# Six changes to the order of VectorE's work in a two-layer transformer trunk

## The chip, the cores and the metric

The kernel runs on one core of one Trainium2 chip. The metric is the device time of one launch in microseconds (us). The kernel before takes 1472.25 us, the median of 3 runs (1472.05 to 1473.08).

## The reference

The program computes a trunk of two layers over 512 latent tokens and 256 context tokens of width 1024, in float32. Cut to what matters for the change:

```
for l in range(2):                                   # layer
    h = modulate(rmsnorm(x, norm1_g[l]), shift, scale)          # shift, scale, gate from c @ w_mod
    z = h @ w_in[l]                                             # q | k | v | u | g
    q = rope(rmsnorm(q, q_norm_g[l])) * 64**-0.5                # 8 heads of 64
    k = rope(rmsnorm(k, k_norm_g[l]))                           # 2 heads of 64
    attn = softmax(q @ k.T) @ v                                 # context sees context only
    g = group_layernorm(gelu(g))                                # 4 groups of 128
    gm = gelu(u) * (w_spatial[l] @ g + b_spatial[l])            # mixes 128 positions
    x = x + gate1 * (concat(attn, gm) @ w_out[l])
    h2 = modulate(rmsnorm(x, norm2_g[l]), shift2, scale2)
    x = x + gate2 * (square(relu(h2 @ w_ff1[l])) @ w_ff2[l])    # 1024 -> 4096 -> 1024
```

In the second layer the context only supplies k and v. The output is the latent stream.

## The kernel before, in words

**Three products for one.** TensorE works on operands that are rounded to a shorter format (fp32r). So every operand is kept as a high part `hi` (a copy in that format) and a low part `lo` (operand less `hi`), and a product is three matmuls: hi by hi, hi by lo, lo by hi. `split` (L220 to L222) makes the two parts: ScalarE copies (L221, `CAST`), VectorE subtracts (L222, `TENSOR_TENSOR`). It serves the weights, in tiles of 128x1024 with a ring of five, and, written out at other lines, the activations: V (L782), the gated mixer `gm` (L795), the softmax weights (L1055), the squared relu (L1179).

**Stages.** Per layer: the input projections (kv, the mixer's u and its four gate tiles g with their layer norm, then q), then attention with the output projection, then the feed-forward layer `ff1`/`ff2` in eight chunks. The second layer begins with the kv projection of the new tokens, which runs into the end of the first layer's feed-forward.

**What sets the order.** The kernel is a program for a scheduler that places each instruction in its engine's row. The code keeps a virtual time and a list of due times (`fl.defer(delay, function)`, delays in the table `PAR`): work such as transposing, mixing and the second matmul group of an attention tile is emitted when its due time has come. In the first layer's feed-forward the rows of VectorE and ScalarE follow the code's order (`manual_schedule`); elsewhere the scheduler decides from its own times. `tc.issue_after(x)`, wrapped as `behind(x)`, keeps an instruction behind another in the row. An engine works through its row in order, so an instruction that waits holds up all behind it.

**Lines that the change touches.**
- `qk` (L699 to L728) takes a PSUM bank with two tiles of q or k. ScalarE squares it (L706), VectorE sums the squares per head (L708, the *reduce*), multiplies the bank by the rotary cosines (L712) and, with halves exchanged, by the sines (L716, two instructions), and adds the two (L717; GpSimd in the second layer). L725 and `rsqrt` (L294 to L311) turn the sums into a factor, and L727 multiplies. After L716 nothing reads the bank any more.
- `make_gm` (L787 to L796) makes the two parts of `gm`. In the first layer the low parts (L795, 128x768) are kept behind the fourth attention tile's maximum (`maxes[3]`).
- `attn_tile`: scores into a `pa` bank, row maximum (L1036), exponential with row sums (L1041), transposes (L1052) and their split (L1054, L1055). After the last of four tiles the sums' reciprocal is taken at once (L1059), and GpSimd spreads it over 128 columns (L1062). It is used later, when the attention product leaves PSUM (L1083, L1085).
- `sink_g` (L878): a gate tile's statistics (`stats`, L888 to L891, then a power on GpSimd at L298), then in `rest` its scaling (L907, four instructions) and its split, then in `mixing` the matmuls and their eviction (L932). L829 and L833 are steps of the gelu of another tile, and L833 is the last reader of that tile's bank.
- `pump` (L238) issues a weight tile's load and both parts of its split; `take` (L284) hands the tile to its user.
- `gate` (L981 to L986) adds a projected bank, times the modulation's gate, to the residual stream X, and thereby frees the bank.
- `ff1_first` and `relu2` (L1169 to L1179): relu and square on ScalarE (L1172, L1177), the square in full precision and its low part on VectorE (L1178, L1179).
- The norms (`Norm`): ScalarE squares X (L477), GpSimd or VectorE adds up (L479), TensorE sums over partitions (L488), `rsqrt`, VectorE copies (L510), TensorE spreads (L515), VectorE multiplies (L526) and takes the low part (L522). `N111` is the due time of the spreading in the second layer's second norm, latter group.

PSUM is held in three pools of banks, `pa` (two banks wide), `pb` and `pt`. A matmul into a bank waits until the last reader of its previous content is done.

## Time and profile before

| | |
|---|---|
| median of 3 runs | 1472.25 us |
| the profiled execution | 1474.03 us |
| span of that execution on the core | 1471.9 us |
| granted TensorE clock | 0.998 |

The profile is of one execution; about 2.1 us of its time lie outside the span. Its rows name an engine, a line, an operation and its operands without the buffer numbers: `X<-pb,modT,X` at L986 is a gate. A row of the timeline has the start from the span's start, the duration, the shape and the count; a row with x2 covers two instructions that follow each other. What stands in brackets is the idle time ahead of the instruction and what ended it. [...]

### The profile page before, as it was taken

How to read it: one execution, taken by the hardware profiler on the slowest of the kernel's cores; microseconds unless marked ns; L12 is line 12 of the kernel's file. 1: busy time of each engine (PE TensorE's matmuls, PEld its weight loads, DVE VectorE, ACT ScalarE, POOL GpSimd, SP SyncE). 2: the span in 40 equal slices, each digit the busy share in tenths (PEclk: the TensorE clock that was granted, in tenths of full speed). 3: DMA queues.
4: the chain of work that ended last, by engine and by line, in shares of the span. 5: the costliest groups of instructions: out<-in, count | busy, mean ns of one | idle time of the engine just before them, and what ended most of it. 6: DMA issues, size and time to landing. Idle time of an engine off the chain costs nothing.

```text
span 1471.9 us, 21047 instructions
## 1 busy us (share of the span) xinstructions
PE 1440.3 (98%) x8178; PEld 1225.0 (83%) x8178; DVE 909.6 (62%) x1594; ACT 642.3 (44%) x1141; POOL 364.6 (25%) x304
## 2 busy tenths in 40 slices
PE   6999999999999999999999999999999999999998
PEld 2899787988888888888888889998889888888887
DVE  5857767778766565655556547777968554444443
ACT  3552546664545452433325234546865323232221
POOL 0323512222256461323324223274121000000000
PEclk9999999999999999999999999999999999999999
DMA  9322443101233343423333212212002322222221
GB/s 367 114 72 92 178 152 143 70 1 57 84 128 122 109 143 99 139 99 136 99 138 118 88 39 74 99 58 72 16 1 73 118 97 100 100 92 95 100 100 57
DMA packets 50083, 148.71 MB, mean 101 GB/s; under 512 B 5440, under 2 KB 6976, under 8 KB 49984
## 3 DMA queue, kind: packets, MB, share of 16 engines
q1 hardware_dynamic: 49408, 146.72, 28.5%
q8 instruction: 64, 1.05, 0.3%
q10 hardware_dynamic: 576, 0.66, 0.1%
q14 instruction: 35, 0.29, 0.1%
HBM read 145.26 MB, written 2.10 MB: 100 GB/s over the span
## 4 chain that ended last, share of the span: by engine, by line
PE 86%; DVE 6%; ACT 3%; POOL 2%; issue 1%; DMA 1%; SPq 0%; POOLq 0%; ACTq 0%; DVEq 0%
PE pa L217 54%; PE pb L217 23%; PE pt L1052 3%; PE pb L354 2%; PE pt L217 2%; POOL m L298 1%; PE pt L745 1%; ACT w L1041 1%; DMA A<-in_w_mod 1%; POOL lo L222 1%; DVE lo L222 1%; ACT hi L221 0%; DVE s L907 0%; ACT A L1054 0%; DVE A L795 0%
## 5 line engine op out<-in xcount | busy, mean ns | idle before, releaser
L217 PE MATMUL pa<-A,hi 128*128 128x512 f32 (+2 forms) x1440 | 430.0, 376 | 0.7 <-DVE s L716 0.4
L221 ACT CAST hi<-raw 128x1024 fp32r<-128x1024 f32 x168 | 176.1, 1049 | 327.7 <-PE pa L217 246.1
L217 PEld LDWEIGHTS pa<-A,hi 128*128 128x128 f32 x1440 | 262.8, 188 | 46.8 <-DVE s L716 0.7
L217 PE MATMUL pa<-A,lo 128*128 128x512 f32 (+2 forms) x832 | 283.8, 347 | 0.0
L222 DVE TENSOR_TENSOR lo<-raw,hi 128x1024 fp32r<-128x1024 f32 x152 | 202.5, 1332 | 122.2 <-ACT hi L221 117.8
L403 POOL TENSOR_TENSOR C<-C,s 128x512 f32<-128x512 f32 x112 | 175.0, 1577 | 295.1 <-ACT s L402 288.3
L217 PE MATMUL pa<-B,hi 128*128 128x512 f32 x750 | 239.0, 391 | 0.0
L217 PEld LDWEIGHTS pa<-A,lo 128*128 128x128 f32 x832 | 156.7, 188 | 21.4
L986 DVE SCALAR_TENSOR_TENSOR X<-pa,modT,X 128x512 f32<-128x512 f32 x168 | 99.8, 615 | 105.6 <-PE pa L217 104.1
L217 PEld LDWEIGHTS pa<-B,hi 128*128 128x128 f32 x750 | 139.9, 188 | 27.1
L217 PE MATMUL pb<-B,hi 128*128 128x512 f32 (+1 forms) x600 | 157.0, 349 | 1.4 <-DVE X L986 1.0
L217 PE MATMUL pa<-B,lo 128*128 128x512 f32 (+1 forms) x450 | 155.2, 354 | 0.0
L986 DVE SCALAR_TENSOR_TENSOR X<-pb,modT,X 128x512 f32<-128x512 f32 (+3 forms) x116 | 70.9, 619 | 79.7 <-PE pb L217 79.7
L217 PE MATMUL pb<-hi,A 128*128 128x256 f32 (+1 forms) x608 | 118.1, 291 | 0.6 <-DVE m L725 0.6
L217 PEld LDWEIGHTS pb<-B,hi 128*128 128x128 f32 x600 | 104.4, 189 | 16.3 <-DVE X L986 2.2
L217 PE MATMUL pb<-B,lo 128*128 128x512 f32 (+1 forms) x300 | 104.2, 347 | 0.0
L217 PEld LDWEIGHTS pb<-hi,A 128*128 128x128 f32 x608 | 96.9, 191 | 2.2 <-PE pb L217 0.8
L217 PEld LDWEIGHTS pa<-B,lo 128*128 128x128 f32 x450 | 84.5, 188 | 14.9
L402 ACT ACTIVATE s<-k,silu 128x512 f32<-128x512 f32 x112 | 77.9, 717 | 34.4 <-DMA k<-in_w_mod 25.3
L217 PE MATMUL pb<-lo,A 128*128 128x256 f32 (+1 forms) x304 | 87.7, 288 | 0.0
L1055 DVE TENSOR_TENSOR A<-pt,A 128x384 fp32r<-128x384 f32 (+1 forms) x144 | 74.0, 537 | 14.6 <-ACT A L1054 12.6
L217 PE MATMUL pb<-A,hi 128*128 128x384 f32 (+2 forms) x288 | 80.4, 360 | 1.1 <-DVE s L833 0.6
(210 smaller groups left out, 2205.1 us busy)
## 6 DMA issues: line engine op xcount, KB each, us to landing
raw<-in_w_ff SPq DMA_DIRECT2D x128, 512.0 KB, 3.5
k<-in_w_mod SPq DMA_DIRECT2D x96, 256.0 KB, 2.8
raw<-in_w_tok SPq DMA_DIRECT2D x16, 512.0 KB, 3.5
raw<-in_w_out SPq DMA_DIRECT2D x16, 512.0 KB, 3.5
lo<-in_w_mod SPq DMA_DIRECT2D x16, 512.0 KB, 4.4
hi<-in_w_mod SPq DMA_DIRECT2D x16, 512.0 KB, 4.0
A<-in_w_mod SPq DMA_DIRECT2D x8, 512.0 KB, 9.9
B<-in_w_mod SPq DMA_DIRECT2D x8, 512.0 KB, 9.5
```

What stands on the lines that cost most here:

```text
L217: pe.matmul(out, a, b, start=start, stop=stop)
L221: act.copy(hi, src)
L222: (eng or vec).tensor_tensor(out=lo, in0=src, in1=hi.bitcast(F32), op=ALU.subtract)
L298: pool_e.tensor_tensor(out=y, in0=v, in1=mhalf[:, 0:n], op=ALU.pow)
L354: pe.matmul(ps[q:q + 32, :], S32[:, k, :], ws_[k2 // 2][:, k2 % 2 * 512:(k2 % 2 + 1) * 512], start=k < ns, stop=k >= KT - ns)
L402: act.activation(p, w, AF.Copy, scale=s)
L403: pool_e.tensor_tensor(out=a, in0=a, in1=p, op=ALU.add)
L745: pe.transpose(p[:, o:o + 128], stk[:, t, hh, c0:c0 + 128].bitcast(F32), ident)
L986: vec.scalar_tensor_tensor(out=xs, in0=src[:, s - off:e - off], scalar=modT[l][:, i * 8 + m, cond:cond + 1], in1=xs, op0=ALU.mult, op1=ALU ...
L1041: act.activation(p, ps[:, 0:nk], AF.Exp, bias=nmx, accum_out=sm)
L1052: pe.transpose(tp_[:, (kt - k0) * 128:(kt - k0) * 128 + 128], p[:, kt * 128:kt * 128 + 128], ident)
L1055: vec.tensor_tensor(out=ptl[:, k0:k0 + step, d], in0=src, in1=pth[:, k0:k0 + step, d].bitcast(F32), op=ALU.subtract)
```

## The change

It changes the order in which work is written or due, and no instruction's operation or shape. VectorE has 1475 rows before and after.

1. `qk`: the products with cosines and sines come first; the reduce over the squares and then the addition follow.
2. `make_gm`, first layer: the low parts are kept behind the eviction of the fifth mixing (`evicted[4]`) instead of the fourth maximum.
3. `attn_tile`: reciprocal and spreading become a function `factors`, due 1200 later.
4. `sink_g`, second layer: of gate tiles with an even number only the statistics are taken at once; scaling and split wait until the next tile, of odd number, is sunk.
5. Weight splits: while `state["gated"]` holds (from the end of a layer's attention to the end of its output projection, and in the first layer's last `ff2` chunk), the copy is issued at once and the low part is put on a list; each `gate` issues one from the list behind itself. `take` issues the low part of its own tile if it is still on the list. `out` weights are excepted.
6. `N111` goes from 3900 to 4600.

```
-       ... "N111": 3900.0 ...
+       ... "N111": 4600.0 ...
...
-            if held is None:
+            if held is None and state.get("gated") and "%s%d" % key[:2] not in PAR["WP"]:
+                act.copy(hi, raw)
+                pend.append((key, lambda hi=hi, lo=lo, raw=raw: vec.tensor_tensor(out=lo, in0=raw, in1=hi.bitcast(F32), op=ALU.subtract)))
+            elif held is None:
                 split(hi, lo, raw, pool_e if "%s%d" % key[:2] in PAR["WP"] else vec)
...
     def take(*key):
+        while any(k == key for k, _ in pend):
+            pend.pop(0)[1]()
...
             ss = small(2 * nh)
-            vec.tensor_reduce(out=ss.rearrange("p (a b) -> p a b", b=nh), in_=sq, axis=AX.X, op=ALU.add)
...
-                (pool_e if l in PAR['R1'] else vec).tensor_tensor(out=t1, in0=t1, in1=t2, op=ALU.add)
+                turning = t2
...
+            vec.tensor_reduce(out=ss.rearrange("p (a b) -> p a b", b=nh), in_=sq, axis=AX.X, op=ALU.add)
+            if tp < 2:
+                (pool_e if l in PAR['R1'] else vec).tensor_tensor(out=t1, in0=t1, in1=turning, op=ALU.add)
...
-                with behind(maxes[3] if l == 0 and len(maxes) > 3 else None):
+                with behind(evicted.get(4) if l == 0 else None):
...
+                elif l and n % 2 == 0:
+                    first()
+                    waiting.append(rest)
+                    fl.defer(PAR["G%d" % l], mixing)
                 else:
+                    while waiting:
+                        waiting.pop(0)()
                     rest()
...
-                    vec.scalar_tensor_tensor(out=xs, in0=src[:, s - off:e - off], ...)
+                    g = vec.scalar_tensor_tensor(out=xs, in0=src[:, s - off:e - off], ...)
+                    if pend:
+                        with behind(g):
+                            pend.pop(0)[1]()
...
                 if hh == qt == 1:
-                    rv = small(4, tag="rv", bufs=2)
-                    vec.reciprocal(rv, st["sm"])
-                    ...
+                    fl.defer(1200.0, factors)
...
+        state["gated"] = True
         with region('aend%d' % l):
             ...
+        state["gated"] = False
...
                 elif end:
+                    state["gated"] = True
                     more(96)
```

Line numbers in the rows of the kernel after are its own: L712, L716, L708, L717 and L725 are now L716, L720, L729, L731 and L732; L795 is L802, L829 and L833 are L836 and L840, L907 is L914, L932 is L939, L1055 is L1071, L1059 is L1080, L1172 and L1177 are L1192 and L1197. The low part of a gated weight is L273.

**VectorE in the first layer's attention over the context.** Before, with the low parts of `gm` (L795) ahead of an eviction of the mixing (L932):

```order
265 L1055 TENSOR_TENSOR A7_324_1904<-pt_325_1905,A6_323_1903 128x2x128
266 L1059 RECIPROCAL rv_333_1945<-sm_292_1804 128x4
267 L891 TENSOR_SCALAR m_341_1970<-mv_340_1961 128x4
268 L795 TENSOR_TENSOR A0_373_2077<-C0_100_482,A0_373_2077 128x768
269 L795 TENSOR_TENSOR A1_374_2080<-C0_100_482,A1_374_2080 128x768
270 L932 SCALAR_TENSOR_TENSOR s_331_1936<-pt_330_1923,gnh_41_173,k2_5_96 128x256 x2
```

and after:

```order
266 L898 TENSOR_SCALAR m_1964<-mv_1955 128x4
267 L1080 RECIPROCAL rv_1997<-sm_1804 128x4
268 L939 SCALAR_TENSOR_TENSOR s_1936<-pt_1923,gnh_173,k_5_96 128x256 x2
269 L1071 TENSOR_TENSOR A_324_1904<-pt_1940,A_323_1903 128x2x128
270 L1102 TENSOR_TENSOR mix_1945<-pb_1946,pv_1951 64x256
271 L442 TENSOR_TENSOR modT_90<-pt_1972,c_70 128x8
272 L1052 TENSOR_REDUCE m_1981<-pa_1978 128x1
273 L1052 TENSOR_REDUCE m_2013<-pa_2010 128x1
274 L914 TENSOR_SCALAR s_1793<-s_1793,mv_1955,m_1966 128x128 x4
275 L367 STREAM_TRANSPOSE s_2029<-pb_1986 128x512
276 L802 TENSOR_TENSOR A_373_2077<-C_100_482,A_373_2077 128x768
```

The eviction now follows the reciprocal directly; the first low part stands eight rows further on, behind a transpose (L362 before), and the second one further still.

**VectorE in the second layer's projections.** Before, with the scaling of a gate tile (L907) ahead of the last step of another tile's gelu (L833):

```order
1005 L891 TENSOR_SCALAR m_8853<-mv_8844 128x4
1006 L222 TENSOR_TENSOR lo_8997<-raw_8994,hi_8996 128x1024
1007 L907 TENSOR_SCALAR s_8838<-s_8838,mv_8844,m_8855 128x128 x4
1008 L833 SCALAR_TENSOR_TENSOR s_8937<-s_8937,pb_8864 128x512
1009 L222 TENSOR_TENSOR B_1498_8861<-s_8838,B_1498_8861 128x512
```

and after:

```order
1005 L898 TENSOR_SCALAR m_8853<-mv_8844 128x4
1006 L222 TENSOR_TENSOR lo_8997<-raw_8994,hi_8996 128x1024
1007 L840 SCALAR_TENSOR_TENSOR s_8930<-s_8930,pb_8857 128x512
1008 L914 TENSOR_SCALAR s_8838<-s_8838,mv_8844,m_8855 128x128 x4
1009 L895 BN_STATS bn_8942<-s_8930 128x6 x2
```

The gelu's step, which frees the bank, has moved ahead of the four scalings.

**ScalarE at the start of the first layer's feed-forward**, where `ff1_first` ends: relu and square of the rows m = 2 (`B2`) and m = 3 (`B3`), and copies of the high parts of weights. Before:

```order
365 L221 CAST hi_882_4379<-raw_881_4377 128x1024
366 L221 CAST hi_887_4425<-raw_886_4423 128x1024
367 L1172 ACTIVATE w_884_4410<-pa_874_4293 128x512
368 L1172 ACTIVATE w_885_4418<-pa_875_4294 128x512
369 L1177 ACTIVATE B2_864_4171<-w_884_4410 128x512
370 L1177 ACTIVATE B3_865_4172<-w_885_4418 128x512
371 L221 CAST hi_890_4431<-raw_889_4429 128x1024
```

and after:

```order
365 L221 CAST hi_882_4378<-raw_881_4376 128x1024
366 L1192 ACTIVATE w_884_4409<-pa_874_4292 128x512
367 L221 CAST hi_887_4424<-raw_886_4422 128x1024
368 L1197 ACTIVATE B2_864_4170<-w_884_4409 128x512
369 L1192 ACTIVATE w_885_4417<-pa_875_4293 128x512
370 L671 DMA w_893_4436<-in_rope 128x256
371 L1197 ACTIVATE B3_865_4171<-w_885_4417 128x512
```

A weight's copy has moved between the relu and the square of m = 2, and that square now stands ahead of the relu of m = 3. The load of the rotary table (L666) has moved up with it. On TensorE, 22 of the 24 matmuls by which `ff1` takes tile m = 4 to the latent columns stood right behind the first four matmuls of `ff2`; they now stand behind the first two row blocks of `ff2`.

## Prediction, made before the changed kernel ran

> **What bounds the kernel now.** I read the page's busy shares first, then what TensorE waited for, then the timeline at each wait that the change can reach. On the page (engine, busy us, share of the span, instructions):

> ```profile
> PE 1440.3 (98%) x8178; PEld 1225.0 (83%) x8178; DVE 909.6 (62%) x1594; ACT 642.3 (44%) x1141; POOL 364.6 (25%) x304
> ```

> TensorE is busy for 1440.3 of 1471.9 us, so no more than 31.6 us of idle time can be had from any reordering. The list of TensorE's waits (line, what it waited for, total us, times, longest) says which of it belongs to VectorE:

> ```profile
> PE pb L354 <- DMA A<-in_w_mod: 12.0, 1, 12.0
> PE pt L367 <- DVE s L932: 1.8, 1, 1.8
> PE pb L217 <- DVE X L986: 1.0, 2, 0.5
> PE pb L217 <- DVE m L725: 0.6, 1, 0.6
> PE pt L1052 <- DVE modT L437: 0.6, 1, 0.6
> PE pb L217 <- DVE s L833: 0.6, 1, 0.6
> PE pa L217 <- DVE A L522: 0.5, 1, 0.5
> PE pa L217 <- DVE s L716: 0.4, 1, 0.4
> PE pt L745 <- DVE m L309: 0.4, 1, 0.4
> PE pb L217 <- DVE s L716: 0.2, 1, 0.2
> ```

> Of the 31.6 us, 12.0 are the first load. The nine VectorE rows here add up to 6.1 us, and a few smaller ones are left out. That is roughly the prize. No operation is removed, so VectorE's work is the same in sum: a wait goes only where VectorE has idle time to put the displaced work in.

> The sum is made against the profiled execution, 1474.03 us; the median of the runs is 1472.25, 1.8 lower, and the difference is carried over to the median unchanged. A measurement of this kernel can tell about 0.2% from no change, 2.9 us.

> **Part 1, products ahead of the reduce.** VectorE, ScalarE's square and TensorE at the first q bank (start, us, instruction, idle before):

> ```profile
> 140.49 0.59 ACT L706 ACTIVATE s<-pb 128x512 f32<-128x512 f32 x1
> 141.11 0.69 DVE L708 TENSOR_REDUCE m<-s 128x8 f32<-128x512 f32 x1 [1.18 <-ACT s L706]
> 142.31 0.75 DVE L716 TENSOR_TENSOR s<-pb,G 128x256 f32<-128x256 f32 x2
> 143.21 0.35 PE L217 MATMUL pb<-hi,A 128*128 128x256 f32 x1 [0.60 <-DVE m L725]
> ```

> VectorE sat idle for 1.18 us until the square was there, then reduced, and only then read the bank, which came free at 143.06; TensorE waited 0.60. The products need the bank, not the square. They can start when the square does, at 140.49, instead of 0.62 later behind its end and another 0.61 later behind the reduce's turn: the bank comes free 1.2 us earlier, twice what the wait needs. What is late next is the factor. Reduce and addition (0.6 each) now follow the products, so its chain starts at 143.06 - 1.2 + 1.2, as before, but with the addition already done; the wait at L745 (0.4) loses perhaps half. I take 0.6 + 0.2 here, 0.4 for the kv bank (`pa`, L716) and 0.3 for the q banks of the second layer (L716, 0.2, and a shorter one). Sum **-1.5**, bounds -1.8 (all the rows named L725, L716 and L745, 1.6, and a little more) and -0.8 (this q bank alone).

> **Part 2, gm's low parts.** In the context's attention:

> ```profile
> 172.40 2.38 POOL L222 TENSOR_TENSOR lo<-raw,hi 128x1024 fp32r<-128x1024 f32 x1
> 173.70 1.11 DVE L891 TENSOR_SCALAR m<-mv 128x4 f32<-128x4 f32 x1
> 174.72 2.06 DVE L795 TENSOR_TENSOR A<-C,A 128x768 fp32r<-128x768 f32 x2
> 176.71 0.86 DVE L932 SCALAR_TENSOR_TENSOR s<-pt,gnh,k 128x256 f32<-128x256 f32 x2
> 177.72 0.25 PE L367 MATMUL pt<-s,c 128*32 128x8 f32 x8 [1.79 <-DVE s L932]
> 187.53 0.18 DVE L1059 RECIPROCAL rv<-sm 128x4 f32<-128x4 f32 x1 [0.69 <-ACT w L1041]
> 188.62 0.30 PE L1052 MATMUL pt<-c,w 128*128 128x128 f32 x1 [0.56 <-DVE modT L437]
> ```

> TensorE waits 1.79 for an eviction that stands behind 2.0 us of low parts. Those gone, the eviction starts at 174.7 instead of 176.7, and the 1.79 goes whole. But both low parts (1.03 each) come back, eight and fifteen rows on. The first falls in a stretch in which VectorE waits for TensorE anyway. The second stands just ahead of the next eviction, where VectorE's idle time is 0.69; 0.34 is left over, and with the row maximum that moves with it I expect the wait at 188.62 to grow by 0.5. **-1.3**, bounds -1.8 (nothing comes back) and -0.8 (1.03 comes back).

> The row L891 also shows what such sums can miss: 1.11 us for four elements per partition, where the same form takes 0.16 elsewhere (below); it ended at 174.81, and a split on GpSimd ended at 174.78. [...]

> **Part 3 and the due time N111.** Reciprocals (0.18 us each) move by one or two rows and their two copies on GpSimd with them; the product that needs them is emitted a further 3100 to 9800 later. Cost nothing, since nobody waits for them; bounds ±0.3, half of the wait at 188.62, the nearest one.

> **Part 4, a gate tile's scaling.** In the second layer's projections:

> ```profile
> 932.97 0.16 DVE L891 TENSOR_SCALAR m<-mv 128x4 f32<-128x4 f32 x1
> 933.04 1.22 DVE L222 TENSOR_TENSOR lo<-raw,hi 128x1024 fp32r<-128x1024 f32 x1
> 935.16 1.11 DVE L907 TENSOR_SCALAR s<-s,mv,m 128x128 f32<-128x128 f32 x4 [0.90 <-POOL m L298]
> 936.19 0.68 DVE L833 SCALAR_TENSOR_TENSOR s<-s,pb 128x512 f32<-128x512 f32 x1
> ```

> L833 frees a bank for which TensorE waits 0.6 (list above). It stood behind four scalings that themselves waited 0.90 for GpSimd's power. Now it goes into that idle time: 0.90 + 1.03 earlier. The scalings come 0.6 later, and the mixing that needs them is due 22100 of virtual time on. **-0.55**, bounds -0.6 and -0.4.

> **Part 5, weight splits behind gates.** Four places, each with its own answer.

> End of the second layer's attention, and its neighbour in kind, the end of the first layer's feed-forward:

> ```profile
> 884.96 1.21 DVE L222 TENSOR_TENSOR lo<-raw,hi 128x1024 fp32r<-128x1024 f32 x1
> 886.62 0.38 PE L217 MATMUL pb<-B,hi 128*128 128x256 f32 x1 [0.46 <-DVE X L986]
> 1108.16 1.22 DVE L222 TENSOR_TENSOR lo<-raw,hi 128x1024 fp32r<-128x1024 f32 x1
> 1109.29 0.87 DVE L986 SCALAR_TENSOR_TENSOR X<-pb,modT,X 128x256 f32<-128x256 f32 x2
> 1109.82 0.39 PE L217 MATMUL pb<-B,hi 128*128 128x256 f32 x1 [0.52 <-DVE X L986]
> ```

> At both, a low part of 1.2 us stands in front of two gates whose banks TensorE needs. At 1109 the gates now come first, which takes the 0.52, and what follows on VectorE runs on earlier into the first `ff1` matmuls, where I put 0.2 on it: **-0.7**, bounds -1.2 (the other gates of that stage too, 1.0 in the list) and 0. At 886 the wait of 0.46 goes too, and perhaps the 0.5 at L522. But the displaced low part is followed, on TensorE, by two gated banks ahead of products that were cover before; that can cost as much as a split and two gates, 1.21 + 0.87 = 2.1. I take **0**, bounds -1.0 and +1.6.

> End of the first layer's attention: three splits move behind gates, and one of them (1.2 us) then stands in front of the next gate, with TensorE's bank behind it; in return every gate of the stage, and with them the norm, is no longer behind those splits. **0**, bounds -0.8 and +1.2, one split or two thirds of one either way.

> The start of its feed-forward is where I expect a loss, because the split that is left over moves TensorE's cover:

> ```profile
> 387.40 1.05 ACT L221 CAST hi<-raw 128x1024 fp32r<-128x1024 f32 x1 [6.87 <-PE pa L217]
> 388.36 1.08 ACT L1172 ACTIVATE w<-pa 128x512 f32<-128x512 f32 x2
> 389.32 0.63 ACT L1177 ACTIVATE B<-w 128x512 fp32r<-128x512 f32 x1
> 388.79 0.39 PE L217 MATMUL pb<-B,hi 128*128 128x512 f32 x1
> 389.02 0.48 PE L217 MATMUL pa<-A,hi 128*128 128x512 f32 x1
> 391.20 1.29 DVE L1179 TENSOR_TENSOR B<-w,B 128x512 fp32r<-128x512 f32 x2
> ```

> Matmuls of this size start 0.23 us apart (388.79 to 389.02). Before, tile m = 4 filled TensorE from 389.02 on, for 24 x 0.23 = 5.5 us, while relu and square of m = 2 and 3 were finished. Now eight matmuls stand between the end of `ff1_first` (four ahead of 389.02, so 388.1) and the first use of m = 2: TensorE gets there at 389.9. The square of m = 2 is delayed by the copy put in front of it (1.05): from 388.36 on relu (0.54), copy (1.05) and square (0.63) now follow each other, to 390.5 with some overlap, where it was 389.95. A wait of 0.6. Six matmuls and the first use of m = 2 later, at 392.1, its low part is needed, and this stands on VectorE behind that copy's own low part: 389.95 + 1.23 + 0.65 + 0.65 = 392.5, a wait of 0.4. **+1.0**, bounds 0 (the scheduler's rows are kept but copy and split come early enough) and +1.7 (m = 3 is late as well).

> **Sum:** -1.5 - 1.3 - 0.55 - 0.7 + 0 + 0 + 1.0 = -3.05. 1474.03 becomes 1470.98, and the median **1469.2 us**. With every bound at its good end it is 7.5 less than before, with every one at its bad end 2.8 more.

> **The rivals.**
> - *The gated splits cost nothing.* The three uncertain places come out at -1.0, -0.5 and 0: -1.5 - 1.3 - 0.55 - 0.7 - 1.0 - 0.5 = -5.55, 1466.7. For it: VectorE is busy 62% and has room; against: at 389 the cover really moves. Chance 0.24.
> - *Nothing comes of it.* TensorE is at 98%, VectorE's work is unchanged, and each wait removed turns up at the next place where VectorE is late, as half of part 2 does: about 1472.3. Against: at 143 and 934 VectorE stood idle at the very time (1.18, 0.90). Chance 0.15. [...]
> - *Splits behind gates collide with the norm's sums*, slower. After each gate comes a square on ScalarE and an addition on GpSimd. Where a split ran beside one, the addition took 1.40 instead of 0.74:

> ```profile
> 1110.42 0.74 POOL L479 TENSOR_TENSOR acc<-acc,s 128x256 f32<-128x256 f32 x1 [2.33 <-ACT s L477]
> 1111.67 1.40 POOL L479 TENSOR_TENSOR acc<-acc,s 128x256 f32<-128x256 f32 x1 [0.51 <-ACT s L477]
> 1111.25 1.23 DVE L222 TENSOR_TENSOR lo<-raw,hi 128x1024 fp32r<-128x1024 f32 x1 [1.09 <-ACT hi L221]
> ```

> Seven splits now stand behind gates, in three norms. If each lengthens its norm's chain by 0.66 and TensorE feels it, that is +4.6; with parts 1, 2 and 4 (-3.35) and the start of the feed-forward (+1.0) the total is +2.3, 1474.5. It decides from four such collisions on (2.6 against 2.35). Against: splits stood beside additions before, too. Chance 0.11.

> **How the numbers follow.** The forecast has 0.50; its own range is 1468.0 to 1470.5, and about half of it lies beyond the 2.9 us. Faster by over 0.2% (below 1469.3): 0.24 + 0.26 = 0.50. Slower by over 0.2% (above 1475.2): 0.07, the upper end of the last rival. Within: 0.43. The range takes in the first two rivals and the forecast and leaves out the far ends: 1465.8 to 1473.6.

> **What would show it.** In the profile after, the waits at L833's and L725's banks and at L367 should be gone from TensorE's list; the reduce should follow the products without 1.18 us of idle time; the wait at L1052 behind L437's should be about 1.1; and near 390 TensorE should wait about 0.6 and 0.4 where it had none. I am wrong if no wait stands there, if the banks after 886 wait for over 2 us, or if GpSimd's additions of 1.4 us lead to new waits at L488 or L515.

## The result, and the profile after

| | before | after |
|---|---|---|
| median | 1472.15 us (4 runs, 1471.73 to 1473.08) | 1483.08 us (4 runs, 1482.36 to 1483.90) |
| profiled execution | 1474.03 us | 1483.59 us |
| span of that execution | 1471.9 us | 1481.8 us |

The ratio is 1.0071, with an interval of 1.0058 to 1.0083: the change makes the kernel 10.9 us slower, where 3.05 less was forecast and the range ended at 1473.6. The page's busy line after:

```profile
PE 1441.9 (97%) x8178; PEld 1228.5 (83%) x8178; DVE 916.5 (62%) x1594; ACT 644.1 (43%) x1141; POOL 364.1 (25%) x304
```

The same 8178 matmuls, busy within 1.6 us of before. So of the 9.9 us that the span gained, 8.3 are time in which TensorE stood still (1481.8 - 1441.9 = 39.9 against 31.6 before) and 1.6 time in which it was busy with the same work for longer. TensorE's list of waits after (line, what it waited for, total us, times, longest), in part:

```profile
PE pb L359 <- DMA A<-in_w_mod: 12.3, 1, 12.3
PE pb L217 <- DVE X L999: 4.0, 2, 2.1
PE pt L752 <- DVE k L740: 2.5, 2, 2.0
...
PE pt L217 <- ACT e L221: 1.7, 1, 1.7
PE pt L217 <- DVE acc L222: 1.7, 1, 1.7
PE pt L426 <- DVE m L421: 1.4, 1, 1.4
...
PE pt L752 <- DVE m L314: 1.1, 1, 1.1
```

What the change aimed at is gone: no row for the eviction (L932, 1.8 before), the gelu's bank (L833, 0.6) or the q bank (L725, 0.6). But the six rows below the first are new or have grown, to 12.4 us in sum. Adding up every wait of 0.15 us or more behind the first 60 us of the timeline gives 13.0 us before and 19.8 after: **+6.7**.

Beside the waits there is the granted clock. Stretches of 10 us (from:to, length, TensorE busy and its instructions, clock), of after and then of before, all in which the clock was under 0.99, but for the kernel's last ones:

```profile
180.00:190.00 10.00, 6.52 (x38) 0.66 0.40 130
340.00:350.00 10.00, 7.92 (x39) 0.98 0.00 0
350.00:360.00 10.00, 10.00 (x51) 0.85 0.33 110
...
990.00:1000.00 10.00, 7.97 (x58) 0.91 0.16 53
1000.00:1010.00 10.00, 10.00 (x44) 0.92 0.15 52
```

```profile
20.00:30.00 10.00, 9.35 (x48) 0.83 1.03 410
170.00:180.00 10.00, 8.21 (x59) 0.91 0.80 308
180.00:190.00 10.00, 8.76 (x63) 0.92 0.47 165
```

What is missing from 1.00, times 10 us, comes to 3.4 + 1.7 + 1.7 = 6.8 after and 1.7 + 1.7 = 3.4 before: **+3.4**, each drop worth 1.7 or twice that, and each right behind a wait of TensorE.

That 6.7 + 3.4 = 10.1 comes so near to the 9.9 of the span is partly luck. The sum of waits leaves out the first 60 us, where they grew by another 1.1, while before's drop at 20 us lies there, behind a wait of 1.8 that stands in after too and brought no drop. And the half clock near 180 ran from 182.4 to 189.3, in part while TensorE stood. So in these two executions the clock accounts for something between the 1.6 of longer work and 3.4: about a third of the loss at most. Over all runs the mean granted clock was 0.994 to 0.995 after, and 0.999 in the 25 runs of the kernel before that were made beside the first experiments. The difference of some 0.004 is at most 5.9 us, or half of the 10.9.

One more row, of the load queue (SP's):

```profile
SPq L264 <- DVE lo L273: 205.0, 11, 79.4
```

A low part that is kept behind a gate also keeps its raw tile, one of two buffers into which weights are loaded. A long wait of this queue is no loss in itself: before, it stood 706.0 us for the low parts (L222) in all, once for 75.0, and after 520.6 for those and 205.0 for these. It matters where the loads run short. At the end of the first attention the queue issued two loads at 337.72 and 343.75 before. After, it issued none until 351.16, just behind a low part that ran at 349.87.

### The profile page after: what moved, and what is told of

It is laid out like the page before. It is cut to its first block, busy times and chain, and to the rows that moved or that the text cites. A ratio compares the mean times of both kernels' runs of the same rounds, so it can differ in the third digit from the quotient of the medians.

```text
span 1481.8 us, 21046 instructions
## 1 busy us (share of the span) xinstructions
PE 1441.9 (97%) x8178; PEld 1228.5 (83%) x8178; DVE 916.5 (62%) x1594; ACT 644.1 (43%) x1141; POOL 364.1 (25%) x304
## 3 DMA queue, kind: packets, MB, share of 16 engines
q8 instruction: 64, 1.05, 0.3%
## 4 chain that ended last, share of the span: by engine, by line
PE 84%; DVE 7%; ACT 3%; DMA 2%; POOL 2%; issue 2%; SPq 0%; POOLq 0%; ACTq 0%; DVEq 0%
PE pa L217 52%; PE pb L217 24%; PE pt L1068 3%; PE pt L217 2%; PE pb L359 2%; PE pt L752 1%; DVE lo L222 1%; DVE A L527 1%; DMA A<-in_w_mod 1%; POOL m L303 1%; POOL lo L222 0%; DVE X L999 0%; DMA hi<-in_w_mod 0%; DVE s L531 0%; ACT w L1057 0%
## 5 line engine op out<-in xcount | busy, mean ns | idle before, releaser
L217 PE MATMUL pa<-A,hi 128*128 128x512 f32 (+2 forms) x1440 | 430.1, 376 | 0.5 <-ACT A L532 0.3
L221 ACT CAST hi<-raw 128x1024 fp32r<-128x1024 f32 x157 | 164.5, 1049 | 322.1 <-PE pa L217 242.1
L217 PEld LDWEIGHTS pa<-A,hi 128*128 128x128 f32 x1440 | 262.8, 188 | 46.8 <-DVE A L527 0.5
L217 PE MATMUL pa<-A,lo 128*128 128x512 f32 (+2 forms) x832 | 283.9, 347 | 1.1 <-DVE lo L273 1.1
L222 DVE TENSOR_TENSOR lo<-raw,hi 128x1024 fp32r<-128x1024 f32 x141 | 191.0, 1354 | 122.9 <-ACT hi L221 118.9
L217 PE MATMUL pa<-B,hi 128*128 128x512 f32 x750 | 239.6, 392 | 0.3 <-DVE X L999 0.3
L217 PEld LDWEIGHTS pa<-A,lo 128*128 128x128 f32 x832 | 156.6, 188 | 23.0 <-DVE lo L273 1.5
L217 PEld LDWEIGHTS pa<-B,hi 128*128 128x128 f32 x750 | 139.7, 188 | 28.4 <-PE pa L217 0.6
L217 PE MATMUL pb<-B,hi 128*128 128x512 f32 (+1 forms) x600 | 158.4, 351 | 4.4 <-DVE X L999 4.0
L217 PE MATMUL pa<-B,lo 128*128 128x512 f32 (+1 forms) x450 | 155.3, 354 | 0.0
L217 PEld LDWEIGHTS pb<-B,hi 128*128 128x128 f32 x600 | 105.2, 190 | 19.2 <-DVE X L999 5.0
L217 PE MATMUL pb<-hi,A 128*128 128x256 f32 (+1 forms) x608 | 118.0, 291 | 0.1
L217 PE MATMUL pb<-B,lo 128*128 128x512 f32 (+1 forms) x300 | 104.7, 349 | 0.0
L217 PEld LDWEIGHTS pb<-hi,A 128*128 128x128 f32 x608 | 96.9, 191 | 1.7 <-PE pb L217 0.3
L217 PEld LDWEIGHTS pa<-B,lo 128*128 128x128 f32 x450 | 84.5, 188 | 14.8
L217 PE MATMUL pb<-lo,A 128*128 128x256 f32 (+1 forms) x304 | 87.6, 288 | 0.0
L1071 DVE TENSOR_TENSOR A<-pt,A 128x384 fp32r<-128x384 f32 (+1 forms) x144 | 73.9, 536 | 16.5 <-ACT A L1070 14.6
L217 PE MATMUL pb<-A,hi 128*128 128x384 f32 (+2 forms) x288 | 81.8, 364 | 0.0
```

The source lines that it names most:

```text
L217: pe.matmul(out, a, b, start=start, stop=stop)
L221: act.copy(hi, src)
L222: (eng or vec).tensor_tensor(out=lo, in0=src, in1=hi.bitcast(F32), op=ALU.subtract)
L1071: vec.tensor_tensor(out=ptl[:, k0:k0 + step, d], in0=src, in1=pth[:, k0:k0 + step, d].bitcast(F32), op=ALU.subtract)
```

## The experiments

All are compared with before on the same chip; the part's lines are those of the diff in front. Differences in us are those of the medians, 1472.92, 1473.03 or 1472.52 for before; the ratio's interval says how sure they are. I first ran the parts apart.

**Part 1 alone** (`qk`'s reduce and addition behind the products):

> The kernel before with part 1 alone (products ahead of the reduce in qk). Own-waits theory (each part brings waits of its own, and a TensorE wait of about 2 us also costs a stretch of half clock): the waits at the first q bank (0.60, 0.39) and the kv bank (0.45) go, but the chain of the factor is late by 1.05 there, by 0.45 at the kv bank and by 2.0 in the second layer's q bank, the last with about 1.7 of clock: +3.5 us, 1475.7. Interaction theory (no part alone is bad, only all together): within 1 us of 1472.2. One-culprit theory (the gated splits do it all): -1.5 us, 1470.7, as predicted.

1474.86, ratio 1.0015 (1.0006 to 1.0024): 1.9 us slower. TensorE's longest waits are 1.80 at 178 (the eviction, as before), 1.85 near 991 at the second layer's q transposes, and 1.06 near 146. The forecast for this part was 1.5 less.

**Part 2 alone** (`gm`'s low parts behind the eviction):

> The kernel before with part 2 alone (gm's low parts behind the fifth eviction). Own-waits theory: the wait of 1.79 goes and two of 1.74 come, both followed by half clock where one was: +0.5 of waits and +1.7 of clock, 1474.4. Interaction theory: within 1 us of 1472.2. One-culprit theory: -1.3 us, 1470.9.

1473.33, ratio 1.0005 (0.9995 to 1.0014): +0.4, no difference that can be told. The wait of 1.79 at the eviction is gone, and one of 1.80 stands at 182.8, for `acc` (L222). I come back to it below.

**Part 5 alone** (`gated` set in all its places, due time N111 as before):

> The kernel before with part 5 alone (weights' low parts behind gates). Own-waits theory: waits of 2.1 (with 1.7 of clock) at the end of the first layer's attention, 1.7 in its feed-forward, 0.9 net at its end and 0.7 net at the end of the second attention: +7.1 us, 1479.3. Interaction theory: at most +2. One-culprit theory: the whole +10.9, 1483.

1486.24, ratio 1.0085 (1.0069 to 1.0102): 13.3 us slower, more than the whole change. The longest wait, TensorE's and the gate that it waited for:

```profile
1125.80 0.80 PE L217 MATMUL pb<-B,hi 128*128 128x256 f32 x2 [3.69 <-DVE X L991]
```

```profile
1125.26 0.48 DVE L991 SCALAR_TENSOR_TENSOR X<-pb,modT,X 128x256 f32<-128x256 f32 x1
```

The gate stands behind the norm's rows (L531 and L527), which fill VectorE from 1118.62 to 1125.3, but for 0.65, with no split among them. Part 5 was to take splits out of the way of gates; it did, and the gates are later.

**Parts 3 and 4 and N111:**

> The kernel before with parts 3, 4 and N111 alone (reciprocal later, even gate tiles' scaling later, due time 4600). All theories: the wait of 0.55 at L833's bank goes and nothing comes: -0.55 us, 1471.6. If it is slower by over 1 us, part of the loss sits here.

1473.83, ratio 1.0007 (0.9998 to 1.0016): +0.9, no difference that can be told. The 0.56 at the gelu's bank is gone, as forecast; 1.24 at the second layer's q transposes (L745, near 988) and 0.89 near 1116 have come. Nothing is won in sum.

**Part 5, place by place.** Only at the end of the first attention (`state["gated"] = l == 0` ahead of that region, and nowhere else):

> Part 5 only at the end of the first layer's attention. Order theory (the splits' new rows make the scheduler move TensorE's work as well, so that TensorE comes to two output-projection banks before VectorE, in the midst of the norm's multiplies, has gated the banks they need): a wait of 2.1 near 349 with up to 1.8 us of clock, and 0.8 to 1.0 twice near 415 and 435 from the split that is left over: +2 to +5 us, 1474.9 to 1478. Split theory (a split in front of the gate makes it late): a split stands between the norm's multiplies and the late gate in the timeline. Clock rival (the loss is mostly the clock): the waits sum to less than a third of the loss.

1477.31, ratio 1.0030 (1.0020 to 1.0041): +4.3. Waits of 2.08 at 348, 0.99 at 413 and 0.81 at 432. Only at the end of the first feed-forward:

> Part 5 only at the end of the first layer's feed-forward. Order theory: 0.46 and 0.49 go, a wait of 1.9 comes for the first of two banks that TensorE reaches early: +0.9 us, and 0 to 1.7 of clock: 1473.8 to 1475.5. My prediction's term was 0.

1475.05, ratio 1.0016 (1.0006 to 1.0025): +2.0. The two waits of 0.46 and 0.48 near 890 are gone, and one of 1.89 for a gate has come. Only at the end of the second attention, with N111 at 4600:

> Part 5 only at the end of the second layer's attention, with N111 at 4600 as in the whole change. Order theory and prediction agree: the wait of 0.52 at the gates goes; -0.2 to -0.7, 1472.2 to 1472.7. With N111 at 3900 part 5 alone had a wait of 3.7 there (at 1125.80); if N111 is what saves it, no wait over 1 us is seen.

1474.74, ratio 1.0012 (1.0003 to 1.0021): +1.7. The 0.52 at the gates is gone, as forecast. The 3.69 is not there either, which I put down to the new due time, since part 5 is the same at this place. What came instead are 0.45 and 0.65 on low parts that TensorE now reaches too early (near 1123 and 1125), and 0.31. These waits, less those that went, are about half of the 1.7; the rest lies within the interval.

The single results of parts 1, 2 and 5 add up to 1.9 + 0.4 + 4.3 + 2.0 + 1.7 = 10.3, near the loss of the whole, 10.9; each is uncertain by 1 to 1.5 us, so that the agreement is better than it had to be. Some 8 us of it are part 5.

**Low parts kept back are let go at a region's end:**

```diff
             fl.run_fillers()
+            while pend:
+                pend.pop(0)[1]()
+        state["gated"] = False
```

> Part 5 alone, but the low parts that are still on the list are issued at the end of each layer's output projection instead of when their tile is taken. Load theory (the low part left over keeps one of the two load buffers and with it the queue of all loads, which makes the modulation late near 435): the waits near 415 and 435 (0.96 and 0.78) go, the others stay: 1.7 less than part 5 alone, 1484.5. Order theory alone: all waits stay, 1486.

This is part 5 as in the third experiment, and no low part outlives the end of an attention. 1480.87, ratio 1.0056 (1.0039 to 1.0073): +7.8 instead of +13.3. The waits near 413 (0.96 in the third experiment, for a gate) and 432 (0.78, for the modulation, L426) are gone; those of 2.08, 1.89 and 3.69 stay. So these two waits in the feed-forward come of a low part left over, and the big waits for gates do not. They are 1.7 of the 5.5 us won. A wait of 0.96 near 998 went too, and the half clock behind the 2.08, which stood in the profiled execution of the third experiment, does not stand in this one's; the two experiments also ran on different chips. The rest of the 5.5 is open.

**The gated weights' low parts at once, on GpSimd:**

```diff
+            if held is None and state.get("gated") and "%s%d" % key[:2] not in PAR["WP"]:
+                act.copy(hi, raw)
+                pool_e.tensor_tensor(out=lo, in0=raw, in1=hi.bitcast(F32), op=ALU.subtract)
```

> Part 5 at the end of the first attention, but with no low part kept back: GpSimd makes the low parts of the gated weights at once, VectorE makes none of them there. TensorE's order comes back to that of before but for one pair of matmuls, while VectorE has the run of modulated rows (L531, L527) in front of the gate of tile 4 without a split in between, as in the version with part 5. Theory 'TensorE's order': the wait of 2.08 was made by two output blocks that TensorE took earlier, with less cover behind them; here it is gone, no wait for a gate (X) is over 0.6 between 335 and 360 us, the waits of 0.99 and 0.81 near 412 and 432 go too, and the time is within 1.5 us of before. Rival 'VectorE's queue': the gate is late since it stands behind that run; then a wait of 1.5 to 2.1 stays and the time is 2 to 4 us above before. [...]

1478.21, ratio 1.0036 (1.0022 to 1.0050): 5.7 us slower, which neither of the theories had. TensorE's waits near the place, and VectorE's and GpSimd's rows at the second of them:

```profile
350.79 0.51 PE L217 MATMUL pa<-A,hi 128*128 128x256 f32 x2 [2.16 <-ACT hi L272]
363.06 1.02 PE L493 MATMUL pt<-ones,acc 128*128 128x1 f32 x8 [1.73 <-DVE acc L484]
```

```profile
360.00 2.37 POOL L273 TENSOR_TENSOR lo<-raw,hi 128x1024 fp32r<-128x1024 f32 x1 [0.71 <-ACT hi L272]
360.68 2.24 DVE L484 TENSOR_TENSOR acc<-acc,s 128x512 f32<-128x512 f32 x1 [0.83 <-ACT s L482]
```

No wait for a gate is left there. TensorE stands 2.16 us for a weight's copy, which stands behind norm rows on ScalarE (349.70, before 346.78). But its order has come back: 19 matmuls of `ff1` stand in front of the output block, as against 17 before and 7 with the low parts behind gates, although VectorE has the same run of norm rows. So TensorE's order follows the low parts, and not the norm rows. The run also shows the price of GpSimd: the addition L484 takes 2.24 us beside the split on GpSimd, against a median of 0.69 for it on VectorE in this run, and TensorE waits 1.73 for the sum. Behind each of the two waits the clock is 0.83 over 10 us, 3.4 us together, of the 7.7 by which this execution (1480.18) is above before's median.

**Part 1 in one layer alone** (the moved lines under `if l == 0`, then under `if l == 1`):

> Part 1 in the first layer alone. Theory 'scratch buffer in the second layer': the loss of part 1 is the wait near 990 us (1.85) where the reduce now stands behind a product that waits for a buffer GpSimd still reads; then this kernel is within 0.7 us of before, its waits near 140 to 190 adding up to about what they were. Rival 'late factor in the first layer': the wait of 1.06 at the transpose near 146 and of 1.00 near 185 carry it; then this kernel is 1.5 to 2.5 above before.

> Part 1 in the second layer alone; TensorE's order is word for word that of before, so all of the difference is VectorE's place. Theory 'scratch buffer in the second layer': a wait of 1.5 to 2 at the transpose (L747) near 990 us, released by the factor on VectorE, against 0.2 at the two places before; 1.5 to 2.2 us above before. Rival 'late factor in the first layer': that wait is made up for by the q banks that come free earlier; within 0.5 us of before.

First layer: 1473.12, ratio 1.0003 (0.9995 to 1.0012), +0.6. Second layer: 1474.49, ratio 1.0012 (1.0004 to 1.0021), +2.0, with TensorE's order that of before throughout. So the loss of part 1 is the second layer's. VectorE and TensorE there (start, us, instruction, idle before), and below them VectorE before:

```profile
987.04 0.76 DVE L718 TENSOR_TENSOR s<-pb,G 128x256 f32<-128x256 f32 x2 [2.66 <-POOL C L945]
987.71 0.68 DVE L730 TENSOR_REDUCE m<-s 128x8 f32<-128x512 f32 x1
988.42 1.10 DVE L733 TENSOR_SCALAR m<-m 128x8 f32<-128x8 f32 x1
989.44 0.68 DVE L741 TENSOR_TENSOR k<-w,k 128x512 fp32r<-128x512 f32 x1
...
990.17 1.09 PE L753 MATMUL pt<-c,k 128*128 128x128 f32 x8 [1.84 <-DVE k L741]
```

```profile
984.14 0.69 DVE L708 TENSOR_REDUCE m<-s 128x8 f32<-128x512 f32 x1 [0.29 <-ACT s L706]
...
987.49 0.76 DVE L716 TENSOR_TENSOR s<-pb,G 128x256 f32<-128x256 f32 x2 [2.06 <-POOL C L937]
988.17 0.58 DVE L725 TENSOR_SCALAR m<-m 128x8 f32<-128x8 f32 x1
988.66 0.68 DVE L733 TENSOR_TENSOR k<-w,k 128x512 fp32r<-128x512 f32 x1
```

In both kernels the product by the sines stands idle for over 2 us, until GpSimd's mixing (L937, L945 here) has read the scratch buffer that the product is to write. Before, the reduce ran ahead of that idle time and cost nothing. Now it follows it. (Some of these rows overlap the next by up to 0.09 us, as 987.04 + 0.76 and 987.71.) Between the start of the sine products and the end of `k`, for which TensorE waits, lay 988.66 + 0.68 - 987.49 = 1.85 us; now it is 989.44 + 0.68 - 987.04 = 3.08. The 1.2 more are the reduce (0.6) and a longer L733 (1.10 against 0.58). The sine products themselves also start later. Counted from 24 matmuls of TensorE (`pt<-ws,B`, at 978.88 here and 980.15 before), it is 8.16 us here and 7.34 before, 0.8 more, because GpSimd's split and with it the mixing ended that much later; why was not taken apart. (The idle times, 2.66 and 2.06, can't be compared, since before the reduce stood ahead of them.) Together that is 2.0, and the wait is 1.84. Another new wait of 0.81 stands near 1004, at the next transposes.

**TensorE halted on purpose.** The kernel before with 14 waits made in the second layer's feed-forward, where the clock is 1.00 and TensorE waits for nothing:

```diff
+                if m in HALT:
+                    d = tw([128, 512])
+                    for j, w in enumerate(HALT[m]):
+                        vec.tensor_copy(d[:, 0:w], ps[:, 0:w] if j == 0 else d[:, 0:w])
+                    halt.append(pe.transpose(pt()[:, 0:128], d[:, 0:128], ident))
...
+        with tc.issue_after(halt[-1].ins) if halt else nullcontext():
+            pe.matmul(out, a, b, start=start, stop=stop)
```

> The kernel before, with 14 halts of TensorE in the second layer's feed-forward, where it otherwise runs at granted clock 1.00 without a wait: after every second block of 24 matmuls VectorE copies a bank's 512 columns one to eight times, and a transpose that needs the copy stands in front of TensorE's next matmuls. By the copies' sizes the waits should run from about 0.5 to 4 us, most of them between 1.2 and 2.5. Theory 'half clock from 1.7 us on': behind most waits over 1.7 us the matmuls start 0.45 instead of 0.23 us apart for up to 3.4 us, behind those under 1.2 none do, so such a wait costs up to 1.7 us more than its length. Rival '3 us': only waits of over 3 us are followed by a half clock; then the drops seen at 180 and 350 in the changed kernel come from several waits close together, not from one. Rival 'chance': drops are as frequent behind short waits as behind long ones.

1531.69, in one execution; the waits are 40.7 of the 58.0 us by which the span is longer. Two of them, and what follows each:

```profile
1267.18 0.30 PE L1230 MATMUL pt<-c,w 128*128 128x128 f32 x1 [2.67 <-DVE w L1229]
...
1268.28 1.05 PE L220 MATMUL pa<-A,hi 128*128 128x512 f32 x2
1269.13 0.63 PE L220 MATMUL pa<-A,lo 128*128 128x512 f32 x1
...
1282.79 0.30 PE L1230 MATMUL pt<-c,w 128*128 128x128 f32 x1 [2.81 <-DVE w L1229]
...
1283.62 0.62 PE L220 MATMUL pa<-A,hi 128*128 128x512 f32 x2
1284.09 0.40 PE L220 MATMUL pa<-A,lo 128*128 128x512 f32 x1
```

Behind the 2.67 the matmuls start (1269.13 - 1268.28)/2 = 0.43 us apart, behind the 2.81 0.23. By wait: 0.39, 0.78, 1.14, 1.34 and 1.80 were followed by no drop; 2.67 by one; 2.81 once by none and once by one; 3.61, and 3.75 twice, by one of 3.41 us; 4.68, 5.14 and 6.07 each by one of twice that length, which began while the wait still ran. So, of these 14, the waits up to 1.8 were harmless and those from 3.6 on always cost; the rival of 3 us falls with the 2.67. But a wait that the kernel itself has near 184, of 1.53, was followed by half clock in the same run, so that 1.8 is no safe length.

In between, the two waits of 2.81 differ in how they lie. In the traces of before, of after and of this run the half clock, but for that at the kernel's end, comes in stretches of 3.41 us or twice that, and within one run their starts lie whole multiples of 3.41 us apart: 46 times in before (21.09 and 178.10), 49 and 190 times in after (182.43, 349.68 and 998.21), and here, with 1267.69, 1318.89, 1335.95 and 1373.50, 15, 5 and 11 times. Cut into such stretches, the time around the 2.81 near 1282 and around the other 2.81, near 1318, looks so (from:to, length, TensorE busy and its instructions, clock):

```profile
1277.93:1281.34 3.41, 2.05 (x10) 1.00 0.35 132
1281.34:1284.76 3.42, 1.97 (x9) 1.00 0.35 113
...
1315.47:1318.89 3.42, 0.61 (x4) 1.00 0.00 0
1318.89:1322.30 3.41, 3.41 (x9) 0.50 0.45 154
```

The first wait is shared by two stretches, and each keeps some 2 us of work. The second lies in one stretch, where 0.61 us of work are left, and the next one runs at half clock. Laid out in the same way, behind the first 60 us and without the kernel's end, these stretches at full clock have the least work: 1.62 in before (from 174.69), and 1.33 (346.27), 1.38 (994.80), 1.55 (899.23) and 1.61 (179.01) in after. All were followed by half clock but the one of 1.55, and no stretch with more work was. So in these two traces the work left in a stretch does not decide alone.

## Why the prediction was wrong

**Part 5, end of the first attention (forecast 0, bounds -0.8 and +1.2; measured +4.3).** The step that failed: I priced splits and gates on VectorE with TensorE's order as it was. I looked for moved cover (the work that fills TensorE until a gate has freed its bank) after 886 and at the start of the feed-forward, and not here. The cover moved here. TensorE and VectorE after, in front of the wait, and then before:

```profile
346.54 0.40 PE L217 MATMUL pa<-A,hi 128*128 128x256 f32 x2
346.77 0.28 PE L217 MATMUL pa<-A,lo 128*128 128x256 f32 x1
346.89 0.64 PE L217 MATMUL pa<-A,hi 128*128 128x256 f32 x4
349.61 1.18 PE L217 MATMUL pb<-B,hi 128*128 128x512 f32 x2 [2.08 <-DVE X L999]
```

```profile
341.70 0.86 DVE L531 SCALAR_TENSOR_TENSOR s<-X,A,pt 128x256 f32<-128x256 f32 x2
...
348.81 0.74 DVE L999 SCALAR_TENSOR_TENSOR X<-pb,modT,X 128x512 f32<-128x512 f32 x1
...
349.87 1.21 DVE L273 TENSOR_TENSOR lo<-raw,hi 128x1024 fp32r<-128x1024 f32 x1
```

```profile
346.56 0.40 PE L217 MATMUL pa<-A,hi 128*128 128x256 f32 x2
...
349.02 0.72 PE L217 MATMUL pb<-B,hi 128*128 128x512 f32 x2
```

```profile
348.22 0.74 DVE L986 SCALAR_TENSOR_TENSOR X<-pb,modT,X 128x512 f32<-128x512 f32 x1
```

Before, TensorE filled the time from 346.56 with 17 matmuls of `ff1` (`pa`) and took the next output block at 349.02, just when its bank came free. After, 7 matmuls stand there, and it is ready at 349.61 - 2.08 = 347.53, 1.49 earlier; and the gate is 0.59 later, for 15 of the norm's rows now stand in front of it where 11 and a split stood. 1.49 + 0.59 = 2.08.

Why the cover went can be read from the order of TensorE's row in the two built programs. Ten of the 17 matmuls now stand behind the output block. The first of them read two low parts and a high part of `ff1`'s weights. These two low parts are the ones that part 5 put behind the gates (L273, the first at 349.87, the second at 351.67), and the high part's load was issued only at 351.16. The others follow them in the row. So the work that had hidden the gate now needs what stands behind the gate. With the low parts made at once on GpSimd, 19 matmuls stood in front again. The waits of 2.08, 0.99 and 0.81 in the run of this place alone are 3.9 of its 4.3, and its profiled execution had no clock drop here.

**The like at 902 and 1126.** At 902 (895 in the run of that place alone; 1.89) all of the wait is lost cover. Counted from TensorE's same matmuls, the gate comes 7.13 us on in both kernels (890.72 to 897.85 before, 895.00 to 902.13 after), but of the matmuls that read the next weight tile 23 stood ahead of the block before, and 2 after. That tile's low part is now made at 903.58, behind the gate, and the others wait their turn behind its user. At 1126, without the new due time (3.69), the gate itself is late: counted from the first `ff1` matmul, it comes 4.15 us later in the third experiment (1121.11 to 1125.26), and 0.09 earlier before (1114.79 and 1114.70), while TensorE is ready for the block no earlier (1.00 us behind that matmul, 0.45 before). Why the norm's rows came ahead of the gate there was not taken apart.

**Part 5, end of the first feed-forward (forecast 0, measured +2.0) and end of the second attention (forecast -0.7, measured +1.7).** The waits named (0.46 and 0.48, 0.52) went. At 886 the upper bound, +1.6, was nearly right and the value taken was not. What failed there was the price of the moved cover, which I had seen: 2.1 at most, taken as 0. At the other end I had counted on a gain of 0.2 in the first `ff1` matmuls; there came waits of 0.45 + 0.65 + 0.31.

**Part 5, start of the feed-forward (forecast +1.0).** No wait stands near 390, so the step was too pessimistic about that place. The low part left over did its harm later: without it the waits of 0.96 and 0.78 near 413 and 432 were gone, 1.7 us.

**Part 1 (forecast -1.5, measured +1.9).** Two steps failed. The first: "The products need the bank, not the square." After, at the first q bank:

```profile
140.12 0.69 DVE L716 TENSOR_TENSOR w<-pb,G 128x512 f32<-128x512 f32 x1 [1.18 <-ACT s L711]
...
141.39 0.68 DVE L729 TENSOR_REDUCE m<-s 128x8 f32<-128x512 f32 x1
```

The very 1.18 us of idle time that the reduce had are now the product's, and the square ends them. All twelve cosine products wait on ScalarE in the built program, this one among them:

```
186 L716 TENSOR_TENSOR w_1350<-pb_1286,G_157 128x512 [waits Activation_49]
```

Both read the same bank, which may be why the program sets one behind the other; that was not tried. The rows of before could not show it, since the reduce waited ahead of the product, but the waits of the built program could have. So the bank came free 0.6 earlier instead of 1.2. That took its wait of 0.60, and the reduce, now behind, gave it back at the transposes (1.05 instead of 0.39): nothing in sum, as the run with the first layer alone shows. The second step: that the reduce costs nothing behind the products. In the second layer it left an idle stretch that had hidden it: +2.0, of which the reduce itself is 0.6.

**Part 2 (forecast -1.3, measured +0.4, no difference).** The eviction's wait went whole, as forecast; what I put on its other side (0.5 at L1052) did not come, and something larger did. ScalarE, GpSimd, VectorE and TensorE after:

```profile
180.06 1.04 ACT L221 CAST hi<-raw 128x1024 fp32r<-128x1024 f32 x1 [2.49 <-PE pa L217]
181.28 0.62 ACT L221 CAST e<-s 128x512 fp32r<-128x512 f32 x1
181.18 2.35 POOL L222 TENSOR_TENSOR lo<-raw,hi 128x1024 fp32r<-128x1024 f32 x1 [4.42 <-ACT hi L221]
181.93 2.15 DVE L222 TENSOR_TENSOR acc<-s,e 128x512 fp32r<-128x512 f32 x1
181.98 0.41 PE L217 MATMUL pt<-ws,e 128*128 128x128 f32 x2 [1.74 <-ACT e L221]
184.13 0.47 PE L217 MATMUL pt<-ws,acc 128*128 128x128 f32 x1 [1.74 <-DVE acc L222]
```

Without the wait for the eviction TensorE comes sooner to work that hangs on `e`. The high part of `e` stands on ScalarE behind a weight's copy, and ScalarE sat idle for 2.49 ahead of that copy. The releaser named (TensorE) had gone on; the copy waited for its load, which was issued at 172.60, landed 7.1 us later at 179.72, and was followed by the copy at 180.06 (178.25 and 178.59 in the run of part 2 alone). The DMA engines were 86% busy between 165 and 183. The low part `acc` then took 2.15 us, 1.6 of them beside GpSimd's split, and 1.15 before, where it ran beside the last 0.6 us of such a split. In the run of part 2 alone it took 2.28, of which 1.7 lay beside one. Why it took longer there was not taken apart. The prediction had such a collision in a rival, with the wrong pair: there it was the norm's additions, here the low part of `acc`.

The wait that came in the run of part 2 alone, 1.80, is as long as the one that went, and it may cost more: the granted clock was 0.996 to 0.998 in all ten runs, against a mean of 0.999 for before, and in the profiled execution half clock follows from 184.35 on, for 6.8 us.

**Part 4 (forecast -0.55).** The wait of 0.6 went. In the run with parts 3 and 4 and N111 waits elsewhere made up for it; which of the three edits brought those was not taken apart.

**The clock** was no term of the sum at all. In the profiled execution two waits of 1.74 with 0.4 us of work between them were followed by a stretch at 0.66, the waits of 2.08 and 2.03 by 1.7 us of loss each. With before's own drops taken off, that is 3.4 us at most.

**The list of waits.** The prediction called the VectorE rows that it left out "a few smaller ones". Three of them are larger than most of those shown (L515 for `modT` 1.8, L1052 for `A` 1.3, L515 for `w` 0.7), and all of VectorE's rows come to some 11.4 us, not 6.1. None of the three lies within reach of the change, so that no term hangs on it.

**The rivals.** "Nothing comes of it" described parts 2 and 4. The rival on the slow side had a collision in the norms, at 1474.5; it missed both mechanism and size. Neither had in it that the low parts put behind a gate are what the work that hides the gate needs.

No version tried beats the kernel before.

## What to carry to other kernels

Where a scheduler places the instructions, moving VectorE's work also moves TensorE's, so look in the order at what covers each wait on the engine that is nearly full, not only at the rows that the edit names. Before putting an operation behind another, ask whether the work that hides this other one needs its result: then the cover goes with it. Before pulling an instruction ahead, read what it waits for in the built program, and what stands in the idle time that it leaves: work that was hidden there is no longer. And a deferred operation holds its input buffer, and with it the queue that fills it, which matters where loads run short: at the end of the first attention the next load was issued at 351.16 here, and at 337.72 before.
